# Fused two-block layer on one core: x and the memory also laid out by rows, relative bias and forget sums spread by way of device memory

## The chip, the cores and the metric

The kernel runs on one core of a Trainium2 chip. Times are device microseconds of one execution, and the median of some executions is compared. TensorE is called PE here, VectorE DVE, ScalarE ACT, GpSimd POOL, and SyncE SP; SP and POOL issue nearly all DMAs.

## The reference

For 256 tokens of width 2048 (T = 256, all float32) two layers are computed one after the other. Only the first block, and the first steps of the cross attention of the second one, are touched by the change:

```python
u = rmsnorm(x, norm_attn)                       # x: (256, 2048)
p = split(u @ w_in)                             # queries, keys, values of four mixers
o_mla = mla_mixer(...)                          # causal softmax, low-rank q and kv
o_fox = fox_mixer(q, k, v, f_logit, b_f)        # s += fcum_i - fcum_j, fcum = cumsum(log_sigmoid(f))
o_nsa = nsa_mixer(..., tbl_nsa)                 # s += tbl[bucket(i - j)]
o_swa = swa_mixer(..., tbl_swa)                 # s += tbl[bucket(i - j)]
h = x + rmsnorm_groups(concat(o_*)) @ w_out     # then an MLP with relu^2
...                                             # second layer: retention, LRU
k, v = rms_norm(mem) @ w_xk, rms_norm(mem) @ w_xv   # mem: (256, 2048)
...                                             # cross attention, PEER experts
```

## The kernel before

All large matrices are streamed from device memory. `Stream.load` issues one DMA on SP for a piece of 1 MB into one of three `raw` buffers. `Stream.split` makes two float32r parts of each half piece: ACT writes the rounded part `whi` (L84), DVE the rest `wlo` (L87). `Stream.run` issues three matmuls for each 128 rows of weights (`whi` with the high part of the activations, `wlo` with it, `whi` with the low part), at most four halves behind the splits.

The activations must have the model width on the partitions: 16 row blocks of 128, kept as eight tiles `xT[0..7]` of [128, 2 parts, 2 blocks, 256 tokens]. The helper `turned` makes such a tile: four PE transposes into PSUM (L269), then ACT writes the high part times the norm's gain (L274), and DVE the low part (L275). `xnorm` does that for x, `mem_prep` for the memory (`mT[0..7]`).

All that isn't a stream of matmuls (softmaxes, norms, transposes) is written as Python generators in the list `Stream.side`. After each half piece `steps` takes two steps of them, and what they emit goes into each engine's queue at that place. `yield "pause"` ends a generator's turn for this half. `until(flag)` runs the generators, with no half pieces between, until a flag is set. Every engine then executes its own queue strictly in the order in which it was emitted; the order is fixed when the program is built, and says nothing of when data are there.

Four places matter here:

- `xnorm`, at the start: SP loads x in four column pieces between the first three weight pieces.
- `rel_bias`: a matmul (L552) makes 16 rows of 384 bias values, ACT copies them to `relrow` (L554), POOL stores them as `reld` in device memory and reads them back in a skewed pattern (`brev`, L564). Row i of the 128 must hold the row shifted by 127 - i; the skewed read gives the shift in the wrong direction, and a matmul with a reversed identity (`anti`, L571) turns the partitions around. The four tiles `bias` are used by `swa` and `nsa` much later; two of them are also sampled at once into `biasc` on DVE (L578).
- `fox_gate` and `fox`: `nF` holds the negated forget sums, [8 heads, 256]; for each of 16 softmax blocks a matmul over 8 partitions (L716) spreads one row over 128 partitions.
- `mem_prep`: POOL loads the memory in four column pieces (`memx`); after the last one the row norm is computed, spread as `Rm` (L254), and the flag `rm` is set. The end of the first column of `w_xv` calls `S.until(lambda: "rm" in have)`.

`mla` waits for the projections `qtm` and `ktm`: DVE applies the rotary factors to `qtm` (L617 to L619), and PE transposes it (L638).

Of the kernel before, what the change touches and what calls it, by code (L numbers as in the profile page):

```python
# [25 lines left out]
CONSTS = [("ident", 128), ("anti", 128), ("tri", 256), ("mask", 256), ("hm", 8), ("cos", 32), ("sin", 32),  # L26
          ("valid", 32), ("iota", 128)]


# [157 lines left out]
class Kernel:  # L187
# [74 lines left out]
    def turned(self, dst, src, kbs, gain=None):  # L262
# [7 lines left out]
        for i, kb in enumerate(kbs):  # L270
# [3 lines left out]
            nc.scalar.activation(hi, q, AF.Copy, scale=gk)  # L274
            nc.vector.scalar_tensor_tensor(lo, q, gk, hi.bitcast(F32), op0=ALU.mult, op1=ALU.subtract)  # L275

    def xe(self, name="xT"):
        return self.g([128, 2, 2, 256], name, F32R)

# [102 lines left out]
    def xnorm(self):  # L382
        nc = self.nc
        ss4, ss = self.small(8, "ss4"), self.small(2, "ss")
        for e in range(8):
            t = self.xe()
            self.turned(t, lambda m, kb: self.x[kb // 4][:, m, kb % 4 * 128:(kb % 4 + 1) * 128],
                        [2 * e, 2 * e + 1], lambda kb: self.gain("norm_attn", kb))
            self.xT[e] = t
            yield  # L390
            if e % 2:
                c = e // 2
                for m in range(2):
                    self.sumsq(ss4[:, m * 4 + c:m * 4 + c + 1], self.x[c][:, m], 512)
# [37 lines left out]
    def block1(self):  # L432
# [25 lines left out]
        xv = t["x"].rearrange("(m p) d -> p m d", p=128)  # L458
        self.x = [self.g([128, 2, 512], "x") for _ in range(4)]
        cut = lambda c, a, b: nc.sync.dma_start(self.x[c][:, :, a:b], xv[:, :, c * 512 + a:c * 512 + b])  # L460
        cut(0, 0, 256)
        cut(0, 256, 512)
        S.load(0, 2)
        cut(1, 0, 512)
        S.load(1, 2)
        cut(2, 0, 512)
        S.load(2)
        cut(3, 0, 512)
# [71 lines left out]
    def rel_bias(self):  # L540


        nc, t = self.nc, self.t
        rel = self.keep([34, 16], "rel")
        nc.gpsimd.dma_start(rel[:32], t["rel_bias"])
        nc.gpsimd.dma_start(rel[32:], t["rel_mask"])
        oh = self.g([34, OHR], "oh")
        nc.gpsimd.dma_start(oh, t["onehot"])
        for _ in range(4):
            yield "pause"  # L550
        p = self.ps()
        nc.tensor.matmul(p[:16, :OHR], rel, oh, start=True, stop=True)  # L552
        b = self.w([16, OHR], "relrow")
        nc.scalar.activation(b, p[:16, :OHR], AF.Copy)  # L554
        d = self.dp.tile([16, OHR], F32, name="reld")
        nc.gpsimd.dma_start(d, b)

        self.biasc = self.keep1([128, 2, 8, 16], "biasc")
        nc.vector.memset(self.biasc, NEG)
        yield  # L560
        self.bias = []
        for a in range(4):
            r, o = self.g([128, 4, 256], "brev"), self.g([128, 4, 256], "bias")
            nc.gpsimd.dma_start(r, bass.AP(tensor=d.tensor, offset=d.offset + 4 * a * OHR,  # L564
                                           ap=[[1, 128], [OHR, 4], [1, 256]]))
            yield
            yield
            yield
            for i in range(2):
                p = self.ps()  # L570
                nc.tensor.matmul(p, self.const("anti"), r[:, 2 * i:2 * i + 2].rearrange("p h j -> p (h j)"),  # L571
                                 start=True, stop=True)
                nc.scalar.activation(o[:, 2 * i:2 * i + 2].rearrange("p h j -> p (h j)"), p, AF.Copy)
                yield
# [104 lines left out]
    def fox_gate(self):  # L679

        nc = self.nc
        yield from self.wait("A1")
        bf = self.bf
        z, lf = self.small(16, "z"), self.small(16, "lf")
        nc.vector.tensor_tensor(z.rearrange("p (m h) -> p m h", h=8), self.PA[1][:, :, 288:296],
                                bf[:, None, :].to_broadcast([128, 2, 8]), op=ALU.add)
        yield from self.log_sigmoid(lf, z, 16)
        yield
        yield "pause"
        tri = self.const("tri")  # L690
        F, nF = self.F, self.nF = self.small(16, "F"), self.w([8, 256], "nF")
# [10 lines left out]
        yield  # L702
        self.have.add("fF")

    def fox(self):
        nc = self.nc
        yield from self.wait("fF", "fq", "fk", "fv")
        F, nF = self.F, self.nF
        o = self.g([128, 2, 512], "o")
        mask = self.const("mask")  # L710
        ready = {}

        def bias(h, m):
            if h not in ready or ready[h][0] != m:
                p = self.ps()
# [176 lines left out]
    def mem_prep(self):  # L892
        nc = self.nc
        self.mT = {}
        mv = self.t["mem"].rearrange("(m p) d -> p m d", p=128)
        ss4, ss = self.small(8, "ss4"), self.small(2, "ss")
        for c in range(4):
            x = self.g([128, 2, 512], "memx")
            nc.gpsimd.dma_start(x, mv[:, :, c * 512:(c + 1) * 512])
            for m in range(2):  # L900
                self.sumsq(ss4[:, m * 4 + c:m * 4 + c + 1], x[:, m], 512)
            yield
            for e in range(2):
                t = self.xe("mT")
                self.turned(t, lambda m, kb: x[:, m, kb % 4 * 128:(kb % 4 + 1) * 128],
                                       [4 * c + 2 * e, 4 * c + 2 * e + 1], lambda kb: self.gain("mem", kb))
# [822 lines left out]
def _consts():  # L1729
    c = {n: np.zeros((128, w), np.float32) for n, w in CONSTS}  # L1730
    c["ident"][:] = np.eye(128)
    c["anti"][:] = np.eye(128)[::-1]
# [35 lines left out]
def lay_out(a):  # L1768
# [6 lines left out]
    for i, (c0, c1) in enumerate(PA_CUTS):  # L1775
# [14 lines left out]
    d["cmp_w2"] = np.ascontiguousarray(np.concatenate([w2, w2], 2))  # L1790
    d["cmp_pos"] = twice(a["nsa_cmp_pos"][0].transpose(2, 0, 1))
    d["x"], d["mem"] = a["x"][0], a["mem_2"][0]
    g = {"norm_attn": a["norm_attn"], "q_norm": a["mla_q_norm"], "kv_norm": a["mla_kv_norm"],
         "group_norm": a["group_norm"], "norm_mlp": a["norm_mlp"], "mix_norm": a["mix_norm_g_2"],
         "ret_gn": a["ret_gn_g_2"], "conv_w": a["conv_w_2"], "conv_b": a["conv_b_2"], "b_rg": a["b_rg_2"],
# [55 lines left out]
```

## Time and profile before

| | |
|---|---|
| median of 3 runs | 3493.42 us (3492.11 to 3496.73) |
| the profiled execution | 3493.89 us, span of its records 3492.1 us |
| granted clock of PE, mean | 0.999 |
| PE busy | 3463.2 us, 99% |
| DVE busy | 2295.6 us, 66% |
| ACT busy | 1655.1 us, 47% |
| POOL busy | 232.5 us, 7% |
| DMA | 703.84 MB, 202 GB/s over the span |

An engine is busy from the first to the last of overlapping instructions; matmuls overlap, so what one costs is read from the distance of the starts around it and not from its duration.

### The profile page before, as it was taken

The numbers are of one execution on the slowest core, as the hardware profiler recorded it, in microseconds if no ns is written. First come the engines' busy times: TensorE is split into PE (matmuls) and PEld (weight loads), VectorE is DVE, ScalarE is ACT, GpSimd is POOL, SyncE is SP. The second block draws the span as 40 slices with busy tenths as digits, with TensorE's granted clock in tenths as the row PEclk, the third lists the DMA queues.
The fourth block names the chain that finished last, engine by engine and source line by source line (L and its number), as shares of the span: only waits on it lengthen the run. The fifth ranks groups of instructions, "written<-read, shape, count | busy, mean of one in ns | idle before, by whom it ended". The sixth has DMA issues, their size and how long they took to land.

```text
span 3492.1 us, 46015 instructions
## 1 busy us (share of the span) xinstructions
PE 3463.2 (99%) x18204; PEld 2950.4 (84%) x18204; DVE 2295.6 (66%) x3476; ACT 1655.1 (47%) x2298; POOL 232.5 (7%) x278
## 2 busy tenths in 40 slices
PE   9999999999999999999999999999999999999998
PEld 7788888888888888878888888888888888888887
DVE  5566565646565566886545789966667677777775
ACT  5455444444343454534434454555555544444443
POOL 0000000000000000000000000123232000000000
PEclk9999999999999999999999999999999999999999
DMA  6544455554545554445545565566666687666664
GB/s 219 177 143 160 175 181 185 192 195 177 198 180 211 192 211 176 174 157 184 207 147 181 195 207 207 200 219 233 221 221 241 238 294 242 242 242 241 242 208 145
DMA packets 112568, 703.84 MB, mean 202 GB/s; under 512 B 12708, under 2 KB 13493, under 8 KB 39392
## 3 DMA queue, kind: packets, MB, share of 16 engines
q1 hardware_dynamic: 87120, 610.98, 49.5%
q0 software_dynamic: 24944, 89.85, 7.5%
q8 instruction: 143, 2.34, 0.3%
q14 instruction: 73, 0.60, 0.0%
q10 hardware_dynamic: 288, 0.07, 0.0%
HBM read 660.98 MB, written 39.87 MB: 201 GB/s over the span
## 4 chain that ended last, share of the span: by engine, by line
PE 92%; issue 4%; DVE 3%; ACT 1%; DMA 0%; POOL 0%; SPq 0%; POOLq 0%; DVEq 0%; ACTq 0%
PE mm L176 30%; PE mm L177 15%; PE mm L166 13%; PE mm L168 13%; PE mm L167 13%; PE ss L1614 2%; DVE wlo L87 1%; PE ss L321 1%; PE ss L269 1%; PE ss L348 1%; PE ss L1362 0%; PE ss L1384 0%; PE ss L333 0%; ACT whi L84 0%; PE ss L796 0%
## 5 line engine op out<-in xcount | busy, mean ns | idle before, releaser
L87 DVE TENSOR_TENSOR wlo<-raw,whi 128x1024 fp32r<-128x1024 f32 (+2 forms) x1162 | 1394.7, 1217 | 676.1 <-ACT whi L84 675.0
L84 ACT ACTIVATE whi<-raw 128x1024 fp32r<-128x1024 f32 (+2 forms) x1162 | 1197.3, 1051 | 637.5 <-PE mm L168 504.2
L176 PE MATMUL mm<-xT,whi 128*128 128x512 f32 x2368 | 845.3, 401 | 0.0
L176 PE MATMUL mm<-fn,whi 128*128 128x512 f32 x2048 | 726.4, 398 | 0.0
L177 PE MATMUL mm<-xT,wlo 128*128 128x256 f32 x2368 | 665.0, 281 | 2.4 <-DVE wlo L87 2.1
L177 PE MATMUL mm<-fn,wlo 128*128 128x256 f32 x2048 | 573.2, 280 | 0.0
L176 PEld LDWEIGHTS mm<-xT,whi 128*128 128x128 f32 x2368 | 445.4, 188 | 107.3 <-issue 1.4
L176 PEld LDWEIGHTS mm<-fn,whi 128*128 128x128 f32 x2048 | 384.5, 188 | 88.2
L177 PEld LDWEIGHTS mm<-xT,wlo 128*128 128x128 f32 x2368 | 447.9, 189 | 5.3 <-DVE wlo L87 4.5
L167 PE MATMUL mm<-wlo,W 128*128 128x512 f32 x1024 | 398.3, 389 | 0.0
L166 PE MATMUL mm<-whi,W 128*128 128x512 f32 x1024 | 398.3, 389 | 0.0
L168 PE MATMUL mm<-whi,W 128*128 128x512 f32 x1024 | 398.3, 389 | 0.0
L177 PEld LDWEIGHTS mm<-fn,wlo 128*128 128x128 f32 x2048 | 386.7, 189 | 0.0
L166 PEld LDWEIGHTS mm<-whi,W 128*128 128x128 f32 x1024 | 192.2, 188 | 40.0
L168 PEld LDWEIGHTS mm<-whi,W 128*128 128x128 f32 x1024 | 192.2, 188 | 39.9
L167 PEld LDWEIGHTS mm<-wlo,W 128*128 128x128 f32 x1024 | 192.2, 188 | 39.8
L166 PE MATMUL mm<-whi,hid 128*128 128x512 f32 x512 | 199.8, 390 | 0.0
L168 PE MATMUL mm<-whi,hid 128*128 128x512 f32 x512 | 199.3, 389 | 0.0
L167 PE MATMUL mm<-wlo,hid 128*128 128x512 f32 x512 | 199.3, 389 | 0.0
L1616 ACT ACTIVATE gst<-ss 128x256 f32<-128x256 f32 x128 | 42.3, 383 | 174.2 <-PE ss L1614 174.2
L168 PEld LDWEIGHTS mm<-whi,hid 128*128 128x128 f32 x512 | 96.1, 188 | 20.1
L166 PEld LDWEIGHTS mm<-whi,hid 128*128 128x128 f32 x512 | 96.1, 188 | 19.8
(506 smaller groups left out, 4011.1 us busy)
## 6 DMA issues: line engine op xcount, KB each, us to landing
raw<-in_peer_u SPq DMA_DIRECT2D x128, 1024.0 KB, 4.9
raw<-in_peer_v SPq DMA_DIRECT2D x128, 1024.0 KB, 4.9
raw<-in_w_up SPq DMA_DIRECT2D x64, 1024.0 KB, 5.0
raw<-in_w_down SPq DMA_DIRECT2D x64, 1024.0 KB, 4.9
raw<-in_w_in_w SPq DMA_DIRECT2D x52, 1024.0 KB, 4.9
raw<-in_w_out SPq DMA_DIRECT2D x32, 1024.0 KB, 4.9
raw<-in_w_in_t SPq DMA_DIRECT2D x22, 1024.0 KB, 4.9
raw<-in_w_xv SPq DMA_DIRECT2D x16, 1024.0 KB, 4.9
```

The lines of the kernel that those rows point to most:

```text
L84: s.nc.scalar.activation(hi[:, :w], raw, AF.Copy)
L87: e.tensor_tensor(lo[:, :w], raw, hi[:, :w].bitcast(F32), op=ALU.subtract)
L166: nc.tensor.matmul(o, xh, w, start=st, stop=False, skip_group_check=True)
L167: nc.tensor.matmul(o, xh, v, start=False, stop=False, skip_group_check=True)
L168: nc.tensor.matmul(o, xl, w, start=False, stop=en, skip_group_check=True)
L176: nc.tensor.matmul(o, w[:, c], xt[:, :, kl], start=st, stop=False, skip_group_check=True)
L177: nc.tensor.matmul(o[:, 0], v[:, c], xt[:, 0, kl], start=False, stop=en, skip_group_check=True)
L269: nc.tensor.transpose(p[:, (2 * i + m) * 128:(2 * i + m + 1) * 128], src(m, kb), self.ident)
L321: nc.tensor.matmul(ps[:, i * kk:(i + 1) * kk], q(h, m), k(h, kk), start=True, stop=True)
L348: nc.tensor.matmul(po[:, i * 64:(i + 1) * 64], PT[:, j * 128:(j + 1) * 128], v(h, kt), start=kt == 0, stop=kt == m)
L1614: nc.tensor.matmul(p[:, j * 128:(j + 1) * 128], o[0][:, j], o[1][:, j], start=True, stop=True)
L1616: nc.scalar.activation(st[i][:, :, 4 * a:4 * a + 4].rearrange("p g t i -> p t g i"), p.rearrange("p (t a g i) -> p a t g i", t=4, a=2, i=8 ...
```

## The change

- x and the memory are given a second time, transposed on the host (`xT`, `memT`), so that a tile of two row blocks is read with 2 KB on each partition. `scaled` replaces `turned` for them: ACT and DVE read the loaded tile, and the transposes are gone. x itself is still needed for its sum of squares; POOL loads it in four pieces, emitted in `xnorm`. `mem_prep` loads both layouts on POOL and has one more `yield` in each of its four rounds.
- `rel_bias` stores every row 128 times ([16, 128, 384]), so that the read can step backwards by one element from copy to copy; the matmuls with `anti` and their copies are gone. The four reads follow the store at once; then come four pauses, and then the samples `biasc`.
- `fox_gate` stores `nF` to device memory and reads it back into two tiles `nFb` that hold each row on all 128 partitions; the 16 matmuls of `fox` are gone.

```diff
+    def scaled(self, dst, src, kbs, gain):
+        nc = self.nc
+        for i, kb in enumerate(kbs):
+            nc.scalar.activation(dst[:, 0, i], src(i), AF.Copy, scale=gain(kb))
+        for i, kb in enumerate(kbs):
+            nc.vector.scalar_tensor_tensor(dst[:, 1, i], src(i), gain(kb), dst[:, 0, i].bitcast(F32),
+                                           op0=ALU.mult, op1=ALU.subtract)
...
-            self.turned(t, lambda m, kb: self.x[kb // 4][:, m, kb % 4 * 128:(kb % 4 + 1) * 128],
-                        [2 * e, 2 * e + 1], lambda kb: self.gain("norm_attn", kb))
+            self.scaled(t, lambda i: self.xr[e // 2][:, e % 2, i], [2 * e, 2 * e + 1],
+                        lambda kb: self.gain("norm_attn", kb))
             self.xT[e] = t
             yield
-            if e % 2:
-                c = e // 2
+            if 1 < e < 6:
+                x[e - 2] = self.g([128, 2, 512], "x")
+                nc.gpsimd.dma_start(x[e - 2], xv[:, :, (e - 2) * 512:(e - 1) * 512])
+            if e > 3:
+                c = e - 4
...
-        cut(0, 0, 256)
-        cut(0, 256, 512)
+        cut(0, 0)
         S.load(0, 2)
-        cut(1, 0, 512)
+        cut(0, 1)
+        cut(1, 0)
         S.load(1, 2)
...
-        d = self.dp.tile([16, OHR], F32, name="reld")
-        nc.gpsimd.dma_start(d, b)
+        d = self.dp.tile([16, 128, OHR], F32, name="reld")
+        nc.gpsimd.dma_start(d, b[:, None, :].to_broadcast([16, 128, OHR]))
...
-            for i in range(2):
-                p = self.ps()
-                nc.tensor.matmul(p, self.const("anti"), r[:, 2 * i:2 * i + 2].rearrange("p h j -> p (h j)"),
-                                 start=True, stop=True)
-                nc.scalar.activation(o[:, 2 * i:2 * i + 2].rearrange("p h j -> p (h j)"), p, AF.Copy)
-                yield
+            o = self.g([128, 4, 256], "bias")
+            nc.gpsimd.dma_start(o, bass.AP(tensor=d.tensor, offset=d.offset + 4 * a * 128 * OHR + 127,
+                                           ap=[[OHR - 1, 128], [128 * OHR, 4], [1, 256]]))
             self.bias.append(o)
+        for _ in range(4):
+            yield "pause"
+        for a, o in enumerate(self.bias):
             if a < 2:
...
+        d = self.dp.tile([8, 256], F32, name="nfd")
+        nc.gpsimd.dma_start(d, nF)
+        self.nFb = [self.g([128, 4, 256], "nFb") for _ in range(2)]
...
-                nc.tensor.matmul(p[:, :256], self.ident[:8, h:h + 1].to_broadcast([8, 128]), nF, start=True, stop=True)
+                p = self.nFb[h // 4][:, h % 4]
...
             x = self.g([128, 2, 512], "memx")
+            r = self.g([128, 2, 2, 256], "memr")
+            nc.gpsimd.dma_start(r, mt[c])
             nc.gpsimd.dma_start(x, mv[:, :, c * 512:(c + 1) * 512])
+            yield
```

On DVE, behind the first softmax blocks of fox (`fb`, `nm`), these rows stood before; the names in brackets are the engines or DMA queues that a row waits for:

```order
L326 ISA nm 128x1
L87 TENSOR_TENSOR wlo<-raw,whi 128x512 [waits DMAHW1_49,Activation_49]
L617 TENSOR_TENSOR rope<-qtm,cst 128x128 [waits Activation_49]
L617 TENSOR_TENSOR rope<-qtm,cst 128x128 x3
L618 TENSOR_TENSOR qtm<-rope 128x8x16 [waits DVE_49]
L619 TENSOR_TENSOR qtm<-rope 128x8x16 [waits DVE_49]
```

In the changed kernel the same place on DVE reads:

```order
L336 ISA nm 128x1
L87 TENSOR_TENSOR wlo<-raw,whi 128x512 [waits DMAHW4_49,Activation_49]
L590 COPY biasc<-bias 128x4x7 [waits DMASW5_49]
L590 COPY biasc<-bias 128x4x15
L590 COPY biasc<-bias 128x4x7 [waits DMASW6_49]
L590 COPY biasc<-bias 128x4x15
L629 TENSOR_TENSOR rope<-qtm,cst 128x128 [waits Activation_49]
L629 TENSOR_TENSOR rope<-qtm,cst 128x128 x3
L630 TENSOR_TENSOR qtm<-rope 128x8x16 [waits DMASW3_49,DVE_49]
L631 TENSOR_TENSOR qtm<-rope 128x8x16 [waits DVE_49]
```

The four samples `biasc`, which wait for the first and the second read of `bias`, now stand ahead of the rotary step of `qtm`; before, the first two stood behind it.

On POOL, the stretch from the forget sums to the reads of the bias is now this (nothing of the first three rows was there before, and `rel` to `oh` were issued some 20 us before the forget sums):

```order
L715 DMA nfd<-nF 8x256 [waits Activation_49]
L718 DMA nFb<-nfd 128x1024 [waits DMASW6_49]
L718 DMA nFb<-nfd 128x1024 [waits DMASW0_49]
L562 DMA rel<-in_rel_bias 32x16 [waits DMASW1_49]
L563 DMA rel<-in_rel_mask 2x16 [waits DMASW2_49]
L565 DMA oh<-in_onehot 34x384 [waits DMASW3_49]
L574 DMA reld<-relrow 2048x1x384 [waits DMASW4_49,Activation_49]
L582 DMA bias<-reld 128x4x256 [waits DMAHW1_49,DMAHW5_49,DMASW5_49,DMASW4_49]
L582 DMA bias<-reld 128x4x256 [waits DMAHW6_49,DMAHW1_49]
```

The store `reld` has 2048 rows of 384 values instead of 16, and the first read waits until it has landed.

On PE, the end of the first column of `w_xv` reads as follows in the changed kernel (`P` are softmax weights of swa, `o` its output, `dg` the diagonal that makes `Rm`, `cx` the inputs of the nsa compression):

```order
L168 MATMUL mm<-whi,mT 128x512
L343 MATMUL ss<-cst,P 128x128 x4
L331 MATMUL ss<-skT,sq 128x256 x2
L343 MATMUL ss<-cst,P 128x128 x4
L358 MATMUL ss<-vmix,PT 128x64 x8
L269 MATMUL ss<-cst,o 128x128 x8
L254 MATMUL ss<-dg,ones 128x256
L814 MATMUL ss<-cx,cw_2785 64x32 x8
L166 MATMUL mm<-whi,mT 128x512
```

Before, the diagonal stood inside that column, between two half pieces:

```order
L168 MATMUL mm<-whi,mT 128x512
L254 MATMUL ss<-dg,ones 128x256
L166 MATMUL mm<-whi,mT 128x512
L167 MATMUL mm<-wlo,mT 128x512
L168 MATMUL mm<-whi,mT 128x512
```

So in the changed kernel the last softmax blocks of swa, the norm and the transposes of its output and the spreading of `Rm` follow one another on PE with no streamed matmul between them.

## Rows read from the trace of the kernel before

**Rows 1.** The page: busy time and share of the span, instructions.
```profile
PE 3463.2 (99%) x18204; PEld 2950.4 (84%) x18204; DVE 2295.6 (66%) x3476; ACT 1655.1 (47%) x2298; POOL 232.5 (7%) x278
```

**Rows 2.** Groups of PE, by form: busy us, mean ns.
```profile
L716 PE MATMUL ss<-nF,cst 8*128 8x256 f32 x32 | 8.6, 396 | 0.0
L571 PE MATMUL ss<-brev,cst 128*128 128x512 f32 x16 | 8.2, 591 | 0.0
```

**Rows 3.** Timeline of PE, 112 to 118 us: start, duration, instructions.
```profile
113.03 1.02 PE L571 MATMUL ss<-brev,cst 128*128 128x512 f32 x2
113.98 1.16 PE L321 MATMUL ss<-fk,fq 64*128 64x128 f32 x8
115.06 1.99 PE L716 MATMUL ss<-nF,cst 8*128 8x256 f32 x8
116.98 0.44 PE L166 MATMUL mm<-whi,cT 128*128 128x384 f32 x1
```

**Rows 4.** Timeline of PE, 17 to 19 us.
```profile
17.16 0.39 PE L167 MATMUL mm<-wlo,xT 128*128 128x512 f32 x1
17.39 0.39 PE L168 MATMUL mm<-whi,xT 128*128 128x512 f32 x1
...
18.52 0.40 PE L168 MATMUL mm<-whi,xT 128*128 128x512 f32 x1
```

**Rows 5.** Timeline of PE, 237 to 239 us.
```profile
237.44 0.60 PE L269 MATMUL ss<-cst,memx 128*128 128x128 f32 x4
237.96 1.13 PE L321 MATMUL ss<-fk,fq 64*128 64x256 f32 x4
```

**Rows 6.** Timeline, 102 to 109 us, the bias chain.
```profile
102.63 0.81 PE L552 MATMUL ss<-oh,rel 34*16 34x384 f32 x2
...
104.25 0.51 POOL L556 DMA_DIRECT2D reld<-relrow  x1 [34.13 <-ACT relrow L554]
```

**Rows 7.** DMA issues: number, KB each, median us from issue to landing.
```profile
brev<-reld POOLq DMA_DIRECT2D x4, 512.0 KB, 7.0
...
reld<-relrow POOLq DMA_DIRECT2D x1, 24.0 KB, 1.8
...
rel<-in_rel_mask POOLq DMA_DIRECT2D x1, 0.1 KB, 1.5
```

**Rows 8.** Timeline of PE, 119 to 125 us; idle time before and its releaser.
```profile
121.92 0.61 PE L638 MATMUL ss<-cst,qtm 128*96 128x128 f32 x4 [0.66 <-DVE qtm L619]
```

**Rows 9.** Timeline of DVE, 112 to 136 us.
```profile
120.47 0.90 DVE L617 TENSOR_TENSOR rope<-qtm,cst 128x128 f32<-128x128 f32 x4 [0.43 <-ACT qtm L481]
...
122.30 0.30 DVE L578 COPY biasc<-bias 128x28 f32<-128x28 f32 x2
```

**Rows 10.** Stretches: length, busy us of PE, PEld, DVE, ACT, POOL; PEclk, DMA share, GB/s.
```profile
10.00:15.00 5.00, 4.89 (x16) 3.94 (x17) 2.94 (x5) 2.13 (x5) 0.00 (x0) 1.00 1.04 411
```

**Rows 11.** Timeline of ACT, 7 to 16 us.
```profile
11.70 1.06 ACT L84 ACTIVATE whi<-raw 128x1024 fp32r<-128x1024 f32 x1 [1.55 <-DMA raw<-in_w_in_t]
```

**Rows 12.** Stretches of 10 us, columns as in rows 10.
```profile
210.00:220.00 10.00, 10.00 (x53) 8.47 (x52) 5.56 (x17) 6.38 (x15) 0.56 (x1) 0.83 0.30 105
```

**Rows 13.** Groups of DVE, first 1000 us: busy us, mean ns.
```profile
L341 DVE COPY PT<-ss 128x512 f32<-128x512 f32 x15 | 10.2, 677 | 3.8 <-PE ss L333 3.8
...
L326 DVE CUSTOM_DVE_ANT_0 s<-ss,bias,sink 128x128 f32<-128x128 f32 (+1 forms) x16 | 5.8, 411 | 3.6 <-PE ss L321 3.6
...
L372 DVE TENSOR_SCALAR o<-o,gr 128x512 f32<-128x512 f32 x8 | 3.5, 481 | 0.6 <-POOL gr L242 0.6
...
L789 DVE COPY cx<-kmix 64x240 f32<-64x240 f32 x8 | 3.0, 369 | 0.1
```

**Rows 14.** Groups of ACT, first 1000 us: busy us, mean ns.
```profile
L328 ACT ACTIVATE P<-s,nm 128x128 f32<-128x128 f32 (+1 forms) x80 | 35.7, 447 | 55.0 <-DVE nm L326 53.5 <-ACT P L328 0.8
...
L260 ACT ACTIVATE junk<-o 128x512 f32<-128x512 f32 x8 | 5.0, 624 | 5.7 <-DVE o L359 3.5 <-DVE o L870 2.1
```

**Rows 15.** Groups of POOL, first 520 us: busy us, mean ns.
```profile
L242 POOL TENSOR_TENSOR gr<-rs,mhalf 128x2 f32<-128x2 f32 x4 | 3.7, 936 | 114.1 <-DVE rs L336 83.3 <-DVE rs L241 30.8
```

More of the change, by code (lines that the diff above doesn't have):

```diff
@@ L25 @@
          ("lam", 8), ("lru_norm", 8), ("xattn", 16), ("mem", 16), ("ffn", 16)]
-CONSTS = [("ident", 128), ("anti", 128), ("tri", 256), ("mask", 256), ("hm", 8), ("cos", 32), ("sin", 32),
+CONSTS = [("ident", 128), ("tri", 256), ("mask", 256), ("hm", 8), ("cos", 32), ("sin", 32),
           ("valid", 32), ("iota", 128)]
@@ L384, in xnorm @@
         ss4, ss = self.small(8, "ss4"), self.small(2, "ss")
+        x = {}
+        xv = self.t["x"].rearrange("(m p) d -> p m d", p=128)
         for e in range(8):
             t = self.xe()
-            self.turned(t, lambda m, kb: self.x[kb // 4][:, m, kb % 4 * 128:(kb % 4 + 1) * 128],
-                        [2 * e, 2 * e + 1], lambda kb: self.gain("norm_attn", kb))
+            self.scaled(t, lambda i: self.xr[e // 2][:, e % 2, i], [2 * e, 2 * e + 1],
+                        lambda kb: self.gain("norm_attn", kb))
             self.xT[e] = t
             yield
-            if e % 2:
-                c = e // 2
+            if 1 < e < 6:
[3 more added lines that the diff above has]
+                c = e - 4
                 for m in range(2):
-                    self.sumsq(ss4[:, m * 4 + c:m * 4 + c + 1], self.x[c][:, m], 512)
+                    self.sumsq(ss4[:, m * 4 + c:m * 4 + c + 1], x[c][:, m], 512)
         nc.vector.tensor_reduce(ss, ss4.rearrange("p (m c) -> p m c", c=4), axis=AX.X, op=ALU.add)
@@ L457, in block1 @@
             S.add(mode="t", pieces=self.wpieces(f"w_in_a{c}", 0, b - a), x=x, end=end_a(c))
-        xv = t["x"].rearrange("(m p) d -> p m d", p=128)
-        self.x = [self.g([128, 2, 512], "x") for _ in range(4)]
-        cut = lambda c, a, b: nc.sync.dma_start(self.x[c][:, :, a:b], xv[:, :, c * 512 + a:c * 512 + b])
-        cut(0, 0, 256)
-        cut(0, 256, 512)
+        self.xr = [self.g([128, 2, 2, 256], "xr") for _ in range(4)]
+        cut = lambda c, e: nc.sync.dma_start(self.xr[c][:, e], t["xT"][2 * c + e])
+        cut(0, 0)
         S.load(0, 2)
-        cut(1, 0, 512)
+        cut(0, 1)
+        cut(1, 0)
         S.load(1, 2)
-        cut(2, 0, 512)
+        cut(1, 1)
+        cut(2, 0)
         S.load(2)
-        cut(3, 0, 512)
+        cut(2, 1)
+        cut(3, 0)
+        cut(3, 1)
         S.loaded = 3
@@ L690, in fox_gate @@
         tri = self.const("tri")
-        F, nF = self.F, self.nF = self.small(16, "F"), self.w([8, 256], "nF")
+        F, nF = self.F, _ = self.small(16, "F"), self.w([8, 256], "nF")
         p = self.ps()
@@ L701, in fox_gate @@
         nc.scalar.activation(nF, p2[:8, :256], AF.Copy, scale=-1.0)
-        yield
+        d = self.dp.tile([8, 256], F32, name="nfd")
+        nc.gpsimd.dma_start(d, nF)
+        self.nFb = [self.g([128, 4, 256], "nFb") for _ in range(2)]
+        for i in range(2):
+            nc.gpsimd.dma_start(self.nFb[i], bass.AP(tensor=d.tensor, offset=d.offset + 1024 * i,
+                                                     ap=[[0, 128], [256, 4], [1, 256]]))
+        for _ in range(3):
+            yield "pause"
         self.have.add("fF")
@@ L707, in fox @@
         yield from self.wait("fF", "fq", "fk", "fv")
-        F, nF = self.F, self.nF
+        F = self.F
         o = self.g([128, 2, 512], "o")
@@ L714, in bias @@
             if h not in ready or ready[h][0] != m:
-                p = self.ps()
-                nc.tensor.matmul(p[:, :256], self.ident[:8, h:h + 1].to_broadcast([8, 128]), nF, start=True, stop=True)
+                p = self.nFb[h // 4][:, h % 4]
                 b = self.w([128, 256], "fb")
@@ L895, in mem_prep @@
         mv = self.t["mem"].rearrange("(m p) d -> p m d", p=128)
+        mt = self.t["memT"].rearrange("(c e) p k t -> c p e k t", e=2)
         ss4, ss = self.small(8, "ss4"), self.small(2, "ss")
@@ L904, in mem_prep @@
                 t = self.xe("mT")
-                self.turned(t, lambda m, kb: x[:, m, kb % 4 * 128:(kb % 4 + 1) * 128],
-                                       [4 * c + 2 * e, 4 * c + 2 * e + 1], lambda kb: self.gain("mem", kb))
+                self.scaled(t, lambda i: r[:, e, i], [4 * c + 2 * e, 4 * c + 2 * e + 1],
+                            lambda kb: self.gain("mem", kb))
                 self.mT[2 * c + e] = t
@@ L1731, in _consts @@
     c["ident"][:] = np.eye(128)
-    c["anti"][:] = np.eye(128)[::-1]
     p = np.arange(128)
@@ L1792, in lay_out @@
     d["x"], d["mem"] = a["x"][0], a["mem_2"][0]
+    for n in ("x", "mem"):
+        d[n + "T"] = np.ascontiguousarray(d[n].T.reshape(8, 2, 128, 256).transpose(0, 2, 1, 3))
     g = {"norm_attn": a["norm_attn"], "q_norm": a["mla_q_norm"], "kv_norm": a["mla_kv_norm"],
```

6 lines of the change are left out of this document (removed).

## The prediction

> **What bounds the kernel now.** I read the page first: PE is busy 99% of the span, every other engine at most 66% [rows 1]. So a matmul that goes saves its own time, and anything that makes PE wait costs it in full. Then I read the groups of PE by form for what is removed, the timeline around such matmuls for what one costs, the DMA issues and the timeline of the bias chain for what takes their place, and the orders of DVE, POOL and PE in both kernels for where a queue now waits. An engine here executes its queue in order, so one row that waits for a DMA holds all rows behind it.
>
> **What is removed.** Durations overlap, so each cost is a distance of starts.
> - `anti`: 8 matmuls, recorded as 16 [rows 2]. One goes from 113.03 to 113.98, 0.95 us [rows 3]; between streamed matmuls a little less, so 0.9. 8 x 0.9 = 7.2 us.
> - Forget sums: 16 matmuls, recorded as 32 [rows 2]. Eight records take 115.06 to 116.98, 0.48 us a matmul [rows 3]; 16 x 0.48 = 7.7 us.
> - x: eight groups of four transposes, the first ahead of all streamed matmuls. In the others three streamed matmuls with a group between them take 18.52 - 17.39 = 1.13 us, and without it 3 x 0.23 = 0.69 (17.16 to 17.39) [rows 4]: 0.44 us, times 7 = 3.1 us.
> - Memory: 237.44 to 237.96, 0.52 us [rows 5], times 8 = 4.2 us.
>
> Together 22.2 us, all on PE. What ACT and DVE do for a tile stays, from another source. The ACT copies that go were hidden under PE and give nothing.
>
> **What is added: the bias store.** It holds 16 x 128 x 384 x 4 bytes = 3.1 MB instead of 24 KB, still from 16 partitions. The first read waits for its landing in POOL's queue, and DVE's first sample `biasc` waits for the reads. Behind that sample stands DVE's rotary step of `qtm`, and behind that the next `wlo`; PE's next row behind the second half of that projection is the transpose of `qtm`. So PE stops there until two bias tiles have landed.
> When does PE get there? Before, the bias matmul starts at 102.63 [rows 6], and PE is ready for the transposes at 121.92 - 0.66 = 121.26 [rows 8], 18.6 us later. Of that two `anti` (1.8 us) and four forget-sum matmuls (1.9 us) go, and four score matmuls of fox are drawn forward (113.98 to 115.06, 1.1 us) [rows 3]: 16.0 us.
> When is the bias there? POOL issues the store 1.6 us after the matmul's start [rows 6]; it takes W to land; the second read is issued 0.8 us behind the first and lands 7.0 us later [rows 7]; two pairs of samples take 0.6 us, and from the start of the rotary step to PE's transposes pass 1.45 us [rows 8, 9]. That is W + 11.5 us. So PE waits W - 4.5 us.
> No row shows W. Lower end: the highest rate here, 411 GB/s [rows 10], gives 7.7 us, and the 1.5 us that 0.1 KB takes [rows 7] make 9.2. Upper end, from the old store of the same buffer on the same queue: 24 KB take 0.3 us more than 0.1 KB [rows 7], so 128 times that is 38 us, with the fixed part 40. I take 30, near the second: it has the same 16 source partitions, while 411 GB/s was reached with 128; the difference of two times of one decimal may well be 0.2 (27 us). So the wait is 25.5 us, less the 0.66 us that was waited there before: 24.8.
> The Trainium skill, SBUF — State Buffer, section "Door 1: The DMA port swizzle", speaks against the change: partitions 0 to 15 reach four of the 16 ports, measured at 104 GB/s for 1 MiB. By an estimate from that page 3.1 MB take 30 us and the sum below stays as it is; no run here shows it yet.
> After so long a wait PE is slow for a while: at 210 to 220 us, after a run of small matmuls, the granted clock is 0.83 [rows 12], 1.7 us lost. I add 1.5 us for one such fall; ends 0 and 3.
>
> **What is moved: the clump at `rm`.** `mem_prep` has four more yields, so `rm` isn't set when the first column of `w_xv` ends, and `until` emits all that is missing in one go. On PE seven rows without a streamed matmul follow, each waiting for the one before through other engines. The chain: two score matmuls 0.6 (four took 1.1 [rows 3]), DVE 2 x 0.41, ACT 0.45, transposes 0.6 (as [rows 5]), DVE copy 0.68, weighted sum 0.5 (like the transposes), DVE division 0.4 (like a score row), square sum 0.62, POOL root 0.94, two DVE scalings 0.96 [rows 13 to 15]: 6.6 us. DVE's samples of `kmix` stand between, four of 0.37 [rows 13], of which the square sum hides 0.6: 0.9. Ten handovers at an estimated 0.1 to 0.2 us: 1.5. Together 9.0 us, in which PE works 1.7: 7.3, and I take 8 with a first wait for P. Ends 4 (samples and handovers hidden) and 12 (the nsa weights that POOL fetches there land late).
>
> **What is moved: the start.** The transposes of the first tile go, and SP has 256 KB less ahead of the fourth weight half, but POOL's four loads of x wait for nothing: they are issued from about 3 us on, 2 MB beside SP's queue, in a stretch where the DMA engines are full (share 1.04) [rows 10]. ACT converts that weight half at 11.70, when it lands [rows 11], and only behind it the second tile of x. If POOL gets half of 411 GB/s, 2 MB of SP's data take 5 us longer; if little, they land 0.6 us earlier. PE has 12 matmuls in hand meanwhile. I take 2 us lost; ends -1 and 6.
> The Trainium skill, DMA: Bandwidth & Descriptors, section "Issuing engines are not separate DMA queues", has DMAs of all issuers interleave on the same 16 engines; by that the loss is nearer to 6 and the sum 4 us more.
>
> **Costed at nothing.** The reads `nFb` land some 10 us ahead of their use; POOL's loads of `rel` and `oh` now queue behind them but have a few us to spare, at worst 3 us. 2 MB more for the memory fall where the DMA engines are half idle [rows 12]; if a buffer comes free late, ACT waits for the landing, 0 to 4 us.
>
> **Sum**, against the profiled execution, 3493.9 us (0.5 above the median of the runs): 3493.9 - 22.2 + 24.8 + 1.5 + 8 + 2 = 3508.0 us.
>
> **Rivals.**
> - *The store is quick* (other side). At W = 9.2 the wait is 4.7 us, and the sum with no fall of the clock is 3493.9 - 22.2 + 4.0 + 8 + 2 = 3485.7. For it: four later 512 KB reads of the same rows land in 7 us [rows 7]. Against it: the rate would have to be that of 128 partitions. It decides below W = 10.
> - *A middling store*, W from 10 to 23: 3487 to 3501, no change that can be told.
> - *The store is slower still, or the start starves too*: W = 40 gives 3518, with 6 us at the start 3522.
> - *DVE never waits there*, since the pauses cover the store: the four pauses span four half pieces, and the 16 us above already contain them; so it is the first rival again.
>
> **How the numbers follow.** 0.2% (7 us) is about what a measurement of this kernel can tell from no change: faster is below 3486.4, slower above 3500.4. The quick store gets 0.10, the middling one 0.22, the forecast (W 23 to 36) 0.53, the slower one 0.15. With the ends of the clump and the start spread over these: faster 0.12, same 0.20, slower 0.68. The range leaves out the quick end and the far tail: 3487 to 3524; that of the likeliest case alone is 3501 to 3516.
>
> **What would show it.** After: no matmuls on `brev` or `nF` and no transposes of x and memory; a store of 3 MB whose time to landing is W, some 30 us; DVE idle before the first `biasc` with a DMA as the releaser, PE idle before the transposes of `qtm` by about 25 us; PE idle around the transposes of swa's output before `Rm`, about 8 us in several pieces; at the start PE waiting for `whi` or the second `xT` for a few us. Wrong would be: W below 10 us; the sample behind the rotary step after all; PE idle elsewhere by more than 5 us, above all at `mT`.

## The result and the profile after

| | before | changed |
|---|---|---|
| median of 6 runs | 3495.07 us (3492.11 to 3499.47) | 3519.95 us (3517.39 to 3522.09) |
| ratio to before | | 1.007, 95% interval 1.006 to 1.008 |
| the profiled execution | 3493.89 us, span 3492.1 us | 3517.39 us, span 3515.6 us |
| granted clock of PE, mean | 0.999 | 0.993 |

The change makes the kernel 0.7% slower. It does take the matmuls away, and still PE ends later. Later in this text the "far mark" is the start of the first matmul on `hid`, which stands behind all side work of the first block: 687.16 us before and 712.37 after, so the loss, 25.2 us, lies wholly ahead of it.

The page's line of busy times, which answers to [rows 1]:

```profile
PE 3445.6 (98%) x18092; PEld 2937.7 (84%) x18092; DVE 2293.2 (65%) x3476; ACT 1649.3 (47%) x2290; POOL 239.5 (7%) x289
```

PE is busy 17.6 us less, in a span that is 23.5 us longer. Where it waits is in the view of waits, PE's part (who waited for whom: us in total, times, longest):

```profile
PE ss L650 <- DVE qtm L631: 28.0, 1, 28.0
PE mm L166 <- ACT whi L84: 8.7, 1, 8.7
PE ss L269 <- DVE o L382: 3.7, 1, 3.7
PE mm L166 <- ACT mT L282: 3.1, 1, 3.1
PE mm L166 <- ACT xT L282: 2.5, 2, 2.0
...
PE ss L650 <- DVE ktm L643: 1.7, 1, 1.7
...
PE ss L343 <- ACT P L338: 1.3, 1, 1.3
```

One wait of 28.0 us stands out; before, the same transposes waited 0.66 us [rows 8]. (The 8.7 us are the wait for the first weight half at the very start. Before, PE waited there 4.3 us for x and 2.7 us for that half, and its first streamed matmul started at 8.85 us; now it starts at 8.72 us.) The DMA issues, which answer to [rows 7] (KB each, median us from issue to landing):

```profile
reld<-relrow POOLq DMA_DIRECT2D x1, 3072.0 KB, 34.9
...
bias<-reld POOLq DMA_DIRECT2D x4, 512.0 KB, 5.3
...
raw<-in_w_ukv SPq DMA_DIRECT2D x2, 256.0 KB, 12.0
```

The store needs 34.9 us: 3.1 MB at 90 GB/s. Its chain is the one of the forecast. POOL's timeline shows the store and, behind 34 us of idling, the reads:

```profile
106.37 1.05 POOL L574 DMA_DIRECT2D reld<-relrow  x1 [10.07 <-ACT relrow L571]
141.50 3.02 POOL L582 DMA_DIRECT2D bias<-reld  x4 [34.09 <-DMA reld<-relrow]
```

DVE's timeline shows the samples, which wait for the reads, with the rotary step of `qtm` behind them:

```profile
145.71 0.30 DVE L590 COPY biasc<-bias 128x28 f32<-128x28 f32 x2 [21.74 <-DMA bias<-reld]
147.20 0.30 DVE L590 COPY biasc<-bias 128x28 f32<-128x28 f32 x2 [1.19 <-DMA bias<-reld]
147.42 0.89 DVE L629 TENSOR_TENSOR rope<-qtm,cst 128x128 f32<-128x128 f32 x4
```

And on PE the transposes of `qtm` start at 148.86 us behind the 28.0 us. The granted clock is in the windows of the stretches in which it was low, and of one while the store ran (columns as in [rows 10]):

```profile
17.40:20.80 3.40, 2.98 (x7) 2.42 (x8) 2.69 (x5) 1.36 (x2) 0.00 (x0) 0.50 1.05 417
...
110.00:120.00 10.00, 9.56 (x60) 8.42 (x60) 4.77 (x16) 3.09 (x9) 0.00 (x0) 1.00 0.97 103
...
148.80:153.90 5.10, 5.04 (x19) 5.05 (x20) 1.28 (x3) 0.60 (x1) 0.00 (x0) 0.50 0.73 251
310.90:314.30 3.40, 3.40 (x8) 2.73 (x9) 1.07 (x3) 0.77 (x1) 0.00 (x0) 0.50 0.85 292
328.00:331.40 3.40, 3.40 (x15) 2.54 (x16) 1.35 (x4) 1.31 (x3) 0.00 (x0) 0.50 0.00 0
```

The clock column is the third from the right: in four of the lines it has 0.50, which is the lower of the two levels (1.2 GHz), each time behind a wait of PE. So there are four falls, not one; at the upper level (2.4 GHz) the same work would have taken PE half of its busy time there. The one fall of the kernel before, at 210 to 220 us [rows 12], is gone.

**The start.** ACT converts the third weight half at 15.06 us; before it did so at 11.70 [rows 11]. Behind it stands the second tile of x, for which PE waits. ACT's timeline:

```profile
15.06 1.06 ACT L84 ACTIVATE whi<-raw 128x1024 fp32r<-128x1024 f32 x1 [5.18 <-DMA raw<-in_w_in_t]
16.02 1.69 ACT L282 ACTIVATE xT<-xr,gains 128x256 fp32r<-128x256 f32 x4
```

The first matmul on `cT` (the input of the low-rank projections) starts at 114.07 us, and before at 111.96. The seven groups of transposes ahead of it are gone (3.1 us by the prediction's working), so the start lost 2.1 + 3.1 = 5.2 us.

**The first column of `w_xv`.** PE's timeline, with the wait for `mT` in its middle and the clump at its end:

```profile
309.58 0.50 PE L166 MATMUL mm<-whi,mT 128*128 128x512 f32 x1 [3.12 <-ACT mT L282]
...
318.47 0.60 PE L343 MATMUL ss<-cst,P 128*128 128x128 f32 x4
319.00 1.13 PE L331 MATMUL ss<-skT,sq 64*128 64x256 f32 x4
321.41 0.93 PE L343 MATMUL ss<-cst,P 128*128 128x128 f32 x4 [1.28 <-ACT P L338]
322.17 2.05 PE L358 MATMUL ss<-vmix,PT 128*128 128x64 f32 x16
327.95 2.15 PE L269 MATMUL ss<-cst,o 128*128 128x128 f32 x8 [3.73 <-DVE o L382]
329.89 1.06 PE L254 MATMUL ss<-dg,ones 128*128 128x256 f32 x2
330.88 1.33 PE L814 MATMUL ss<-cx,cw 128*64 128x32 f32 x16
332.14 0.50 PE L166 MATMUL mm<-whi,mT 128*128 128x512 f32 x1
```

From 318.47 to 332.14 us no streamed matmul runs. The clump has 1.3 + 3.7 us of waits and 1.7 us of slow clock (half of 3.4). The wait for `mT` takes 3.1 us, 0.5 more for its low part, and 1.7 of slow clock. It isn't a wait for a load: the load of the last piece of the transposed memory (`memr`) was issued at 281.21 us, none of the four took more than 8.1 us to land, and ACT wrote this `mT` only from 309.04 us, behind a softmax of swa.

**The sum at the far mark:** -22.2 removed, +27.3 for `qtm` (28.0 - 0.66), +2.5 for the slow clock behind it, -0.5 for `ktm` (2.2 before, 1.7 now), +5.2 start, +5.3 `mT`, +6.7 clump, -1.7 because the fall at 210 to 220 us [rows 12] is gone: +22.6 us. Measured are +25.2; 2.6 us are not accounted for.

### The profile page after: what moved, and what is told of

Its sections match the earlier page's. It is cut to its first block, busy times and chain, and to the rows that moved or that the text cites. A ratio compares the mean times of both kernels' runs of the same rounds, so it can differ in the third digit from the quotient of the medians.

```text
span 3515.6 us, 45814 instructions
## 1 busy us (share of the span) xinstructions
PE 3445.6 (98%) x18092; PEld 2937.7 (84%) x18092; DVE 2293.2 (65%) x3476; ACT 1649.3 (47%) x2290; POOL 239.5 (7%) x289
## 4 chain that ended last, share of the span: by engine, by line
PE 89%; issue 6%; DVE 3%; ACT 1%; DMA 1%; POOL 0%; SPq 0%; POOLq 0%; DVEq 0%; ACTq 0%
PE mm L176 29%; PE mm L177 15%; PE mm L166 13%; PE mm L168 13%; PE mm L167 13%; PE ss L1636 2%; DVE wlo L87 1%; PE ss L331 1%; PE ss L358 1%; PE ss L269 1%; DMA raw<-in_w_in_t 1%; PE ss L1384 0%; PE ss L1406 0%; ACT whi L84 0%; PE ss L343 0%
## 5 line engine op out<-in xcount | busy, mean ns | idle before, releaser
L177 PE MATMUL mm<-xT,wlo 128*128 128x256 f32 x2368 | 664.5, 281 | 2.4 <-DVE wlo L87 2.3
L177 PE MATMUL mm<-fn,wlo 128*128 128x256 f32 x2048 | 571.9, 279 | 0.0
L177 PEld LDWEIGHTS mm<-xT,wlo 128*128 128x128 f32 x2368 | 447.2, 189 | 5.0 <-DVE wlo L87 4.3
L177 PEld LDWEIGHTS mm<-fn,wlo 128*128 128x128 f32 x2048 | 386.3, 189 | 0.0
```

Of the source, the lines that this page charges most:

```text
L177: nc.tensor.matmul(o[:, 0], v[:, c], xt[:, 0, kl], start=False, stop=en, skip_group_check=True)
```

## The experiments

All were timed against the kernel before, whose medians beside them are 3494.0 to 3494.9 us.

**late_sample**: the samples are taken in `nsa`.

```diff
 # rel_bias
-        for a, o in enumerate(self.bias):
-            if a < 2:
-                for m, n in ((0, 7), (1, 15)):
-                    nc.vector.tensor_copy(self.biasc[...], o[...])
         self.have.add("bias")
 # nsa
         nc.vector.reciprocal(gt, gt)
+        for a, o in enumerate(self.bias):
+            if a < 2:
+                for m, n in ((0, 7), (1, 15)):
+                    nc.vector.tensor_copy(self.biasc[...], o[...])
         yield
```

> The four samples of the bias are taken in nsa, some 200 us later; the store of 3 MB and its reads stay as they are. Placement theory: PE's 28.0 us before the transposes of qtm were DVE's sample alone, so the wait falls to the 0.7 us of before and the slow clock behind it goes (2.5 us): about 3490 us, 30 less than the changed kernel. Rival, the store itself is in the way: while it runs the DMA engines are busy (share 0.97 to 1.00 at 103 to 146 GB/s), so weight pieces land late and PE waits for whi and wlo instead, 10 to 25 us: 3500 to 3515.

Measured: 3503.36 us, 1.003 (1.0018 to 1.0042) of before: 16.6 us less than the changed kernel, and not 30. PE's waits (L646 here is L650 of the changed kernel):

```profile
PE ss L646 <- DVE ktm L639: 5.9, 1, 5.9
PE ss L646 <- DVE qtm L627: 4.8, 1, 4.8
```

The store still takes 34.9 us, and now ACT waits for weights in it (`whi` stands ahead of `ktm` in its queue). ACT's timeline:

```profile
129.57 0.63 ACT L84 ACTIVATE whi<-raw 128x512 fp32r<-128x512 f32 x1 [5.41 <-DMA raw<-in_w_ukv]
...
136.60 2.00 ACT L84 ACTIVATE whi<-raw 128x1024 fp32r<-128x1024 f32 x2 [4.12 <-DMA raw<-in_w_in_w]
```

So both theories hold in part: the place of the sample makes PE wait, and the store also holds up the weight stream. Together the two waits are 10.7 us instead of 29.7, and the sample's place alone is worth 16.6 us of the time.

**wide_store**: the bias matmul writes each row to 8 partitions.

```diff
+        rep = self.w([34, 16, 8], "relrep")
+        nc.vector.tensor_copy(rep, rel[:, :, None].to_broadcast([34, 16, 8]))
-        nc.tensor.matmul(p[:16, :OHR], rel, oh, start=True, stop=True)
+        nc.tensor.matmul(p[:128, :OHR], rep.rearrange("k h r -> k (h r)"), oh, start=True, stop=True)
-        nc.gpsimd.dma_start(d, b[:, None, :].to_broadcast([16, 128, OHR]))
+        nc.gpsimd.dma_start(d.rearrange("h (r c) o -> (h r) c o", r=8),
+                            b[:, None, :].to_broadcast([128, 16, OHR]))
```

> The matmul writes every bias row to 8 partitions, and the store of the same 3 MB goes out of 128 partitions instead of 16; the samples stay where they are. Source theory: the time to landing is set by the 16 source partitions, so it falls from 34.9 to 8 to 12 us, PE's wait at qtm to 1 to 5 us, and the time to 3490 to 3495. Rival, volume and number of pieces (2048 of 1536 bytes each) set it: 30 to 35 us as before, and 3515 to 3520.

Measured: 3497.40 us, 1.0009 (1.0000 to 1.0018). The DMA issues:

```profile
reld<-relrow POOLq DMA_DIRECT2D x1, 3072.0 KB, 11.5
...
raw<-in_w_ukv SPq DMA_DIRECT2D x2, 256.0 KB, 4.9
```

The same bytes in the same 2048 pieces land in 11.5 us instead of 34.9, so neither volume nor pieces set the 34.9 us; reading them out of 16 partitions did. (Each of these is read 128 times, and each of the 128 only 16 times; the run doesn't tell the two apart.) The Trainium skill, SBUF — State Buffer, section "Door 1: The DMA port swizzle", says that the partitions a transfer touches decide how many of 16 ports serve it; the trace agrees, with 90 GB/s out of 16 partitions and 273 GB/s out of 128; the page's 104 GB/s, from which the prediction estimated 30 us, was not reached. `w_ukv` lands in 4.9 us instead of 12.0, so the neighbours of the store are quick again too. PE's wait for `qtm` falls from 28.0 to 6.4 us.

**wide_late** has both edits, and **wide_late_pace** also turns the four pauses of `rel_bias` into steps that count:

```diff
-        for _ in range(4):
-            yield "pause"
+        for _ in range(4):
+            yield
```

> Store from 128 partitions and samples in nsa, both. Fox theory: PE still waits 4 to 5 us for qtm, since with the steps of the removed matmuls gone eight softmax blocks of fox stand ahead of qtm on ACT and DVE instead of four; about 3496. Rival: the 4.8 us that were left with the samples moved came from the long store, so with both edits the wait is under 1.5 us: about 3491.

> As wide_late, and the four pauses of rel_bias are plain yields, so that each takes one of the two steps of its half piece, as the removed matmuls did, and fox again sends four softmax blocks ahead of qtm. Fox theory: PE's wait for qtm falls under 1.5 us and the slow clock behind it goes: 4.8 and some 2 us less, about 3490. Rival: as wide_late.

Measured: 3495.67 us, 1.0003 (0.9994 to 1.0012), and 3498.21 us, 1.0009 (1.0000 to 1.0018). PE's waits in wide_late:

```profile
PE ss L650 <- DVE qtm L631: 4.8, 1, 4.8
...
PE ss L650 <- DVE ktm L643: 1.7, 1, 1.7
```

and in wide_late_pace:

```profile
PE ss L650 <- DVE ktm L643: 3.9, 1, 3.9
...
PE ss L650 <- DVE qtm L631: 2.7, 1, 2.7
```

The 4.8 us are there with a short store as well, so they are not the store's. They come from fox: the steps of the removed matmuls are free, so the second tile of fox is drawn forward, and eight softmax blocks of 0.6 us each stand ahead of `qtm` on ACT and DVE instead of four. But the fox theory falls in its second half: with the old pace the wait moves from `qtm` to `ktm`, 6.6 us together against 6.5, and nothing is won. Before, both waits made 2.9 us. In this stretch PE runs up against ACT and DVE in either order, and about 3.6 us of the removed matmuls come back as waits. That wide_late_pace is even 2.5 us above wide_late by the medians (the intervals overlap) fits another row of its profile, the window of the clump at `rm`:

```profile
297.90:311.50 13.60, 9.70 (x44) 8.54 (x45) 6.26 (x23) 3.33 (x12) 3.03 (x6) 0.50 0.26 84
```

PE works 9.7 us there at the lower level; in wide_late only one stretch of 3.4 us of the clump is low.

**three_yields**: `mem_prep` without the added yields, and **mem_only**: the kernel before with the memory part alone, in this form.

```diff
             nc.gpsimd.dma_start(x, mv[:, :, c * 512:(c + 1) * 512])
             yield
-            for m in range(2):
-                self.sumsq(ss4[:, m * 4 + c:m * 4 + c + 1], x[:, m], 512)
-            yield
             for e in range(2):
+                if e:
+                    for m in range(2):
+                        self.sumsq(ss4[:, m * 4 + c:m * 4 + c + 1], x[:, m], 512)
                 t = self.xe("mT")
```

> The four added yields of mem_prep are taken out (the square sums stand with the second tile of a round). Yield theory: both the clump at rm (some 7 us) and the wait of 3.1 us for mT with its slow clock (5.3 us together) come from mem_prep being four yields late, so both go: about 3508, 12 less than the changed kernel. Rival: the wait for mT comes from the loads, which wait for buffers, so only the clump goes: about 3513.

> The kernel before with the memory part alone, without added yields. Full gain of the transposes: 4.2 us, about 3490.5. Rival: the doubled loads make mT late (a wait of 1 to 4 us) or the moved square sums hold ACT: no change, 3493 to 3496.

Measured: 3512.47 us for three_yields, 1.0055 (1.0041 to 1.0069), 7.5 less than the changed kernel. The waits for `mT` and for `o` are both gone from PE's list, so the yields made both, and the rival (late loads) falls. It isn't 12 us because swa's softmax, which no longer falls into a clump, waits elsewhere. PE's timeline and the window behind it:

```profile
311.32 1.07 PE L343 MATMUL ss<-cst,P 128*128 128x128 f32 x4 [3.10 <-ACT P L338]
```

```profile
312.00:318.80 6.80, 6.80 (x17) 4.68 (x17) 4.00 (x11) 3.43 (x8) 0.00 (x0) 0.50 0.11 48
```

3.1 us instead of 1.3 for P, and 6.8 us at the low clock. The store also took 36.4 us in this execution, and the wait for `qtm` 29.5. mem_only gives 3493.04 us, 0.9992 (0.9983 to 1.0001): 1.9 us less by the medians, not enough to tell from nothing or from the 4.2 expected. PE's list has no wait for `mT` there.

**x_behind** and **x_later** move POOL's loads of x to SP, behind the third and behind the fourth weight piece.

```diff
 # x_behind: block1, behind cut(3, 1)
+        for c in range(4):
+            nc.sync.dma_start(self.x[c], xv[:, :, c * 512:(c + 1) * 512])
 # x_later: xnorm
-            if 1 < e < 6:
-                nc.gpsimd.dma_start(x[e - 2], xv[:, :, (e - 2) * 512:(e - 1) * 512])
-            if e > 3:
-                c = e - 4
+            if e == 3:
+                for c in range(4):
+                    nc.sync.dma_start(x[c], xv[:, :, c * 512:(c + 1) * 512])
+            for c in {5: (0,), 6: (1,), 7: (2, 3)}.get(e, ()):
```

> The four loads of x for the square sums are issued by SP behind the transposed tiles and the first three weight pieces, instead of by POOL at once. Sharing theory: POOL's 2 MB took their part of the DMA engines while PE waited for the third weight half and the second tile (15.06 us instead of 11.70), so PE reaches the relative-bias matmul about 5 us earlier and the time is about 3515. Rival: the transposed tiles on SP themselves are late, or the square sums now wait for x on ACT: 3518 to 3523.

> The changed kernel with the loads of x issued by SP behind the fourth weight piece, and the square sums taken behind the sixth to the eighth tile. Volume theory: at the start 2 MB more have to pass full DMA engines than before (about 5 us at 400 GB/s), whoever issues them, so only a later place mends it: the first matmul on cT comes at 109 instead of 114 us and the time is about 3515. Rival: the square sums are then late for the end of the first projection, which waits for r, and nothing is won: 3518 to 3523.

Measured: 3522.70 us for x_behind, 1.0079 (1.0065 to 1.0092), so no gain. ACT's timeline:

```profile
11.36 1.06 ACT L84 ACTIVATE whi<-raw 128x1024 fp32r<-128x1024 f32 x1 [1.62 <-DMA raw<-in_w_in_t]
...
27.78 1.06 ACT L84 ACTIVATE whi<-raw 128x1024 fp32r<-128x1024 f32 x1 [7.70 <-DMA raw<-in_w_in_t]
```

The third half is back at 11.36 us, but the seventh, of the fourth piece, comes only at 27.78, and PE waits 5.2 us there for the tile behind it. So not POOL is to blame, but 2 MB more ahead of the fourth piece. By the Trainium skill, DMA: Bandwidth & Descriptors, section "Issuing engines are not separate DMA queues", DMAs run on the same 16 engines and interleave, whichever engine started them; the trace agrees, with 3522.70 us when SP issues the 2 MB ahead of the fourth piece and 3519.95 us when POOL does. x_later takes 3514.19 us, 1.0052 (1.0038 to 1.0066), 5.8 less than the changed kernel: the first matmul on `cT` stands at 109.20 instead of 114.07 us, 2.8 ahead of before, as seven groups of transposes should give (3.1).

**fox_only** and **bias_only**: the kernel before with the forget sums alone, or with the bias alone in its mended form (the edits of wide_late).

> The kernel before with one part of the change: the forget sums are spread by way of device memory, the 16 matmuls of fox go. If all of a removed matmul is won, 7.7 us: about 3487. Chain theory: ahead of qtm and ktm PE already waited for ACT and DVE (0.7 and 2.2 us), so the matmuls that go ahead of these places come back there as waits, and 3 to 5 us are won: 3490 to 3492.

> The kernel before with the bias part alone, in its mended form: store of every row 128 times out of 128 partitions, samples in nsa, no matmuls with anti. Full gain: 7.2 us, about 3487.5. Chain theory: the steps that go draw four more softmax blocks of fox ahead of qtm, whose 2.4 us on ACT and DVE come back as a wait of 3 to 4 us with a slow clock behind it: 3490 to 3494.

Measured: 3491.32 us for fox_only, 0.9988 (0.9979 to 0.9997), 3.6 less than before, in the range of the chain theory. But its profile shows another place too, PE's timeline:

```profile
245.56 1.09 PE L269 MATMUL ss<-cst,memx 128*128 128x128 f32 x4 [4.25 <-DMA memx<-in_mem]
```

Here PE waits for a load of the memory. PE came to these transposes at 241.3 us, 5.3 us earlier than before, but the load was also issued later, as POOL's timeline shows, in the kernel before and in fox_only:

```profile
238.60 0.73 POOL L899 DMA_DIRECT2D memx<-in_mem  x1 [17.73 <-ACT mT L274]
```

```profile
240.92 0.73 POOL L905 DMA_DIRECT2D memx<-in_mem  x1 [21.59 <-PE mm L177]
```

By its releaser it waited for a buffer that PE's streamed matmuls (L177) still read; the two new tiles `nFb` come from the same pool of buffers, which is the likely reason, though no run tests it. The wait for `qtm` is 1.7 us, that for `ktm` 2.2 as before. So part of the gain is given back, but not only at `qtm` and `ktm` as I had it. The profiled execution is the slowest of its eleven (3493.21 us), and what this load cost in the others isn't shown.

bias_only: 3499.45 us, 1.0014 (1.0005 to 1.0023), slower by 4.5 us although 7.2 us of matmuls went. Its wait for `qtm` is 1.5 us only, less than expected. The loss is in PE's timeline and in the windows:

```profile
115.04 2.23 PE L711 MATMUL ss<-nF,cst 8*128 8x256 f32 x8
117.20 2.07 PE L321 MATMUL ss<-fk,fq 64*128 64x128 f32 x8
119.21 3.77 PE L711 MATMUL ss<-nF,cst 8*128 8x256 f32 x8
```

```profile
116.70:126.90 10.20, 10.20 (x30) 8.26 (x29) 4.74 (x22) 4.27 (x17) 3.02 (x4) 0.50 0.95 313
...
140.60:147.40 6.80, 6.80 (x20) 5.29 (x20) 4.08 (x10) 3.57 (x7) 0.00 (x0) 0.50 0.13 52
```

PE is busy all the time there, and its clock is at the lower level for 17 us, which costs half of that, 8.5 us. The second tile of fox, drawn forward, puts two groups of scores and forget-sum matmuls behind one another: 8 records of `nF` took 1.99 us in [rows 3] and 3.77 here. There is also a wait that the kernel before doesn't have, for a softmax of swa at 299.18 us:

```profile
PE ss L333 <- ACT P L328: 2.9, 1, 2.9
```

Behind it the clock is low for another 3.4 us (1.7 us lost). With this wait, and less the fall at 210 to 220 us that is gone (1.7), it makes 8.5 + 2.9 + 1.7 - 1.7 = 11.4 us; 7.2 us won and 4.5 lost want 11.7. So the chain theory named a right cause (fox drawn forward) and the wrong price (the clock in the main, not the wait for `qtm`), and it didn't see the wait at swa; what brought that wait isn't tested.

**all_mended** (wide_late_pace, three_yields and x_later together) and **mended_no_pace** (the same with pauses):

> All mends together: store from 128 partitions, samples in nsa, plain yields in rel_bias, no added yields in mem_prep, loads of x later. If the causes add up: 3490 less 7.5 for mem_prep and 5 for the start, about 3478; the kernel before less the 22 us of removed matmuls would be 3472. If they hide one another, waits come back elsewhere: 3482 to 3492.

> All mends but the plain yields in rel_bias (pauses as in the change). If the plain yields only moved the wait from qtm to ktm and lost a little at the clump, 2 to 3 us less than with them: about 3479. Rival: no difference, 3481.

Measured: 3481.19 us, 0.9957 (0.9943 to 0.9971), and 3482.49 us, 0.9964 (0.9951 to 0.9978): both faster than either kernel, and not to be told apart, so the rival of the last expectation holds. PE's waits in all_mended:

```profile
PE ss L650 <- DVE ktm L643: 3.9, 1, 3.9
PE ss L650 <- DVE qtm L631: 2.8, 1, 2.8
```

Here the far mark stands at 674.38 us, 12.8 ahead of before. Of the 22.2 us 3.8 come back as longer waits at `qtm` and `ktm`; two stretches of 3.4 us at clock 0.50 (from 118.1 and 131.7 us) against one before cost 1.7; 3.9 us I can't place.

## Why the prediction was right and where it was off

Direction and main cause were right; the time was not: 3508.0 forecast, 3519.95 measured. That is inside the range but above the 3501 to 3516 of the likeliest case alone. With the measured W the prediction's own sum gives 3512.9. That the time is still inside the range is in part luck: its upper part was there for a store of 40 us (3518, and 3522 with 6 us at the start), while what lies above 3512.9 came from `mT` and the clock as well as from the start. Against the terms of the sum:

- **The store and the wait for `qtm`:** shown. W was taken as 30 us between 9.2 and 40, and is 34.9. The wait was to be W - 4.5 = 30.4 for this W; it is 28.0, since the reads landed sooner (5.3 us instead of 7.0) and from landing to transposes 7.6 us pass (141.3 to 148.86) instead of 9.85. PE was ready 16.1 us after the bias matmul (104.74 to 120.87), forecast 16.0. So 24.8 became 27.3, within the term's bounds, and what made W is the source (wide_store).
- **What the forecast left out of that chain:** that without the sample PE would wait for `qtm` anyway, 4.8 us. I had the four score matmuls drawn forward as 1.1 us of PE, and not their softmaxes, 2.4 us on ACT and DVE ahead of `qtm`. Hidden behind the store it cost the sum nothing. Nor does it upset the wait of the rivals with a quicker store: wide_store, with W = 11.5, waits 6.4 us for `qtm`, and W - 4.5 is 7.0. For such a W the prediction's sum, without a fall of the clock, is 3493.9 - 22.2 + 6.3 + 8 + 2 = 3488.0; that wide_store is level with before instead comes from the other terms below, which the sum had too small or not at all.
- **The clock:** "1.5 us for one such fall" was the wrong count: there are four. Behind `qtm` it was 2.5 us, and each of the three other waits brought 1.5 to 1.7 more, which I count with their places.
- **The start**, 2 us (ends -1 and 6): mis-sized, 5.2 us. The upper end was near, and my reason for taking less, the 12 matmuls in hand, was wrong: they cover one late half, not 2 MB more through full DMA engines (share 1.04 [rows 10]). x_behind and x_later show that the volume ahead of the fourth piece counts, and not the issuer.
- **`mT`, "costed at nothing":** the step that failed. I looked at landings (0 to 4 us), but 5.3 us were lost because `mem_prep` was four yields late: the stream demanded the next tile, its steps came out behind swa's softmaxes, and ACT made it last. The loads had landed long before (above), and three_yields takes the wait away with the same loads. It is the mechanism of the clump, which I saw at `rm` and not one tile earlier. The prediction's own sign of being wrong, more than 5 us of idle at `mT`, was not reached by the idle time alone (3.6 us), only with the slow clock behind it.
- **The clump at `rm`**, 8 us (4 to 12): 6.7 by the rows, right in place and near in size. Its removal together with `mT` gave 7.5 us, not 12.0, so the price of a wait in the profile is not what its removal wins.
- **Removed matmuls**, 22.2 us: in the mended kernel 12.8 us are won at the far mark. That each of them "saves its own time" at 99% busy holds for the transposes of x (2.8 of 3.1 us) and not for fox (3.6 of 7.7) and the bias (4.5 lost), behind which PE next meets ACT and DVE, a load or the lower clock. For the memory it isn't settled (1.9 of 4.2 us, within the noise).

Together: +5.3 `mT`, +3.2 the start, +2.5 the wait for `qtm`, +1.0 the clock behind it, -0.5 `ktm`, -1.3 the clump, -1.7 the old fall that is gone, 8.5 of the 12 us. 2.6 us are those not accounted for at the far mark, and the rest lies between the profiled executions and the medians.

## What to carry to other kernels

In a queue that is fixed in advance, ask of each transfer that you make longer not only who waits for it but what stands behind that waiter, and from how many partitions it is read: with the same bytes out of 128 partitions and the sample moved, 24 of the 25 us were gone (22.6 with the store alone, 16.6 with the sample alone). A removed step also removes its place in the schedule, so look at what is drawn into it, and at flags that now come late; one yield per round cost 7.5 us here. A busy share of 99% does not promise that a removed matmul is won in full: the next wait on the path, or the lower clock, can take its part back, and a tile that takes its place may take a buffer that a load needs.

## What the runs showed of the hardware

- The DMA engines read as full while they moved little. With the store under way, from 110 to 120 us, the changed kernel's windows show share 0.97 at 103 GB/s (the second line in the fence of windows above), while 1.04 came with 411 GB/s in [rows 10]; and 256 KB of `w_ukv` took 12.0 us beside it (4.9 beside the wide store, 2.6 before). So the store out of 16 partitions slowed its neighbours, and the share alone didn't tell how much was moved.
- The granted clock fell to 0.50 while PE was at work: at 210 to 220 us of the kernel before [rows 12], after 10 us with PE busy throughout, and in bias_only at 116.7 us, with one gap of 0.45 us in the 6.7 us ahead of it. Each time scores and forget-sum matmuls stood just ahead. It also differs from run to run: in mem_only it is 0.50 at 131.8 to 135.2 us, behind a wait of 2.15 us for `ktm` that both kernels have, and ahead of all that this kernel changes (its first load of the memory is issued at 222.6 us); the kernel before had 1.00 there. The mean over an execution is 0.999 in the profile of the kernel before and 0.996 to 0.998 in 27 later executions of it. So a microsecond or two between two profiles need not be an effect of an edit.
